# Layer 0's experts: one planner fixes each engine's order, context's output products are grouped, its rows are added as quarter rows, and GpSimd computes nothing there

## The chip, the cores and the metric

The kernel runs on one core of a Trainium2 chip. Its time is the device time of one execution in microseconds (us), as the median of three runs. One further execution was profiled; the rows below come from that one.

## The reference, cut to what matters

Two transformer layers over 1024 image tokens (`x`) and 256 context tokens (`ctx`), width 1024. Each layer ends in 16 experts. An expert takes the tokens with the highest affinity to it (128 of `x`, and in layer 0 also 32 of `ctx`), runs them through a gated hidden layer of 1024 and adds the gated result to their rows:

```python
cap = CAPACITY_FACTOR * t // N_EXPERTS
...
xs = jax.vmap(lambda hb, ib: hb[ib])(h, idx)
hid = jax.nn.silu(jnp.einsum('becd,edf->becf', xs, wg)) * jnp.einsum('becd,edf->becf', xs, wu)
ys = jnp.einsum('becf,efd->becd', hid, wd) * gates[..., None].astype(h.dtype)
return jax.vmap(lambda ib, yb: jnp.zeros((t, d), h.dtype).at[ib.reshape(-1)].add(yb.reshape(-1, d)))(idx, ys)
```

In layer 0 this is called for `x` and for `ctx` with the same expert weights; in layer 1 for `x` alone.

## The kernel before, in words

**Weights.** The three matrices of an expert (`wg`, `wu`, `wd`, 4 MB each in float32) come as six pieces of 2 MB, in the order wg0, wu0, wg1, wu1, wd0, wd1 (0 and 1 are the halves of the hidden width for wg and wu, of the hidden rows for wd). `Experts.dma` fetches a piece on SP's queue into one of three staging tiles `wst`. `Experts.split` cuts each into four units and makes two float16 tiles of a unit: ScalarE writes `wh` (L47), VectorE the rest `wl` (L55). There are 24 units in a ring, one expert's worth. So a staging tile is free when ScalarE and VectorE have split it, and a unit when TensorE has used it.

**One expert (`moe`, layer 0, 160 columns).** GpSimd gathers the token rows `xg` by indirect DMA (L80). TensorE transposes them (L92, 32 transposes `pt`, copied to `xT` at L94 by VectorE and ScalarE in turn). For each of eight blocks `f` of the hidden width, 48 products go into one PSUM tile `pgu` (L117, two tiles in rotation): float16 high and low parts of both factors, three terms. ScalarE computes silu into `sg` (L119), VectorE the product `hd` (L120), GpSimd the high part `hh` (L121) and the low part `hl` (L122). Then the output products: 24 steps (eight `f`, three terms). In each step come two products of 512 columns for the 128 image tokens (`py`, L138) and four of 256 columns for the 32 context tokens (`pc`, L141), each of which uses 32 of the array's 128 columns, side by side (`tile_position=(0,32*g)`). VectorE scales `py` into `ys` (two instructions, L147) and `pc` into `yc` (four instructions of 32 rows, L154), and GpSimd adds both to the tokens' rows `xr` and `cr` in memory by indirect DMA (L149, L155).

**What sets the order.** In this stage the framework's scheduler decides in which order each engine's instructions stand, from its own timeline; each engine has one list of its own. `Plan` (L936) is already in the kernel for another stage: work is handed to it as operations with an engine, a cost, what they read and write, a due time `v` and, for a PSUM tile, `get` and `free`. `Plan.order` is a list scheduler over those costs: among the operations that could start nearly as early as the earliest on an engine it takes the one with the lowest due time. `Plan.emit` records them in the resulting order and ties each instruction to the one before it on its engine.

Of the kernel before, what the change touches and what calls it, by code (L numbers as in the profile page):

```python
# [12 lines left out]
WS=256.0  # L13
CF=0
class Experts:
# [16 lines left out]
    def dma(self):  # L32
        e,m,c=self.todo.pop(0); nc=self.tc.nc
        p,r,NS=self.sts[self.m%len(self.sts)]; self.m+=1
# [36 lines left out]
def moe(tc, streams, E, ident, ahead=None, LD=5, fin=None):  # L71
# [3 lines left out]
    with tc.tile_pool(name="mx",bufs=2) as px, tc.tile_pool(name="mps",bufs=2,space=SP_) as ps, contextlib.ExitStack() as ec:  # L75
# [21 lines left out]
        if ahead: ahead()  # L97
        if len(streams)>1: pcp=ec.enter_context(tc.tile_pool(name="mpc",bufs=1,space=SP_,side="right"))
        xT=[t for t in turn(xg,True)][0]
        for e in range(nE):  # L100
# [30 lines left out]
            for ds in halves:
                for f in range(8):
                    if f%4==0 and ds[0]==0: E.upto(6*e+4+f//4+LD); D[f//4]=E.piece(e,2,f//4)
                    wh,wl=D[f//4][f%4]
                    n=0
                    for a,b in ((0,wh),(1,wh),(0,wl)):
                        for d in ds:
                            nc.tensor.matmul(py[d],hv[a][:,f,0:128],b[:,d*512:(d+1)*512],start=(f==0 and n==0),stop=(f==7 and n==2))  # L138
                        if pc is not None:
                            for g in range(4):  # L140
                                nc.tensor.matmul(pc[32*g:32*g+32,:],hv[a][:,f,128:160],b[:,g*256:(g+1)*256],start=(f==0 and n==0),stop=(f==7 and n==2),tile_position=(0,32*g))  # L141
                        n+=1
            def tokens():
# [6 lines left out]
            def context():  # L150
                s=streams[1]
                yc=px.tile([32,1024],F32,name="yc",bufs=1)
                for g in range(4):
                    last=nc.vector.scalar_tensor_tensor(yc[:,g*256:(g+1)*256],pc[32*g:32*g+32,:],s['gate'][32*g:32*g+32,e:e+1],s['g2'][32*g:32*g+32,g*256:(g+1)*256],op0=OP.mult,op1=OP.mult)  # L154
                return last,nc.gpsimd.indirect_dma_start(out=s['x'],out_offset=bass.IndirectOffsetOnAxis(ap=s['idx'][:,e:e+1],axis=0),in_=yc,in_offset=None,compute_op=OP.add)  # L155
# [780 lines left out]
class Plan:  # L936

    LAT=dict(PE=0.25,DVE=0.12,ACT=0.15,POOL=0.2,SP=2.7)
    def __init__(self,tc,kinds): self.tc,self.kinds,self.ops=tc,kinds,[]; self.W,self.R={},{}; self.last={}
# [507 lines left out]
```

## Time and profile before

| | us |
|---|---|
| median of three runs | 3189.5 (3186.51 to 3199.17) |
| the profiled execution | 3186.68 |
| its span, first to last instruction | 3184.9 |
| first to last add of `ys` in layer 0's experts | 427.6 to 1139.1 |

A row of the timeline gives the start, the duration, the engine, the line, the operation and its operands; `x4` is four instructions in one row. A row with PEld is a load of weights into the array, one with PE a product. Idle time before a row stands in brackets with what ended it.

### The profile page before, as it was taken

Reading aid. Unit: us, or ns where it says so; the run is one execution under the profiler, and the core shown is the slowest. Engines: PE = TensorE matmul, PEld = TensorE weight load, DVE = VectorE, ACT = ScalarE, POOL = GpSimd, SP = SyncE. Lnnn points to the kernel's source line nnn. Section 1 sums busy time; section 2 is a strip of 40 time slices with the busy share of each in tenths; the row PEclk is TensorE's granted clock in tenths of the full one; section 3 lists DMA queues with packets and bytes.
Section 4 is the critical chain, followed back from the end, with each engine's and each line's share of the span. In section 5 each row is a group of like instructions: output and inputs, shape, how many; then the busy total and the mean of one; then the engine's idle time right before and its main releaser. Section 6 shows DMA issues by size and latency. Waiting matters only on the chain.

```text
span 3184.9 us, 76806 instructions
## 1 busy us (share of the span) xinstructions
PE 2725.4 (86%) x31812; PEld 1968.7 (62%) x31812; DVE 2425.0 (76%) x4001; ACT 1965.4 (62%) x3386; POOL 1330.2 (42%) x1326
## 2 busy tenths in 40 slices
PE   3898499999999979998988689999758399888987
PEld 1323367667667644676655678888724177777775
DVE  4657877777776757688989588888788788778787
ACT  3214555555555547677656467777655677677775
POOL 4447343333433325566877100000000466566664
PEclk7899699999999989999875679999878699999999
DMA  6677788888888732322556746666445399999997
GB/s 243 233 264 247 263 319 281 296 302 284 300 303 271 250 109 109 120 69 72 176 160 180 141 82 115 125 118 128 135 154 198 135 353 347 334 338 348 352 347 264
DMA packets 468001, 705.63 MB, mean 222 GB/s; under 512 B 148889, under 2 KB 254781, under 8 KB 467650
## 3 DMA queue, kind: packets, MB, share of 16 engines
q1 hardware_dynamic: 451650, 644.08, 61.5%
q0 software_dynamic: 16000, 56.64, 6.5%
q8 instruction: 249, 4.08, 0.5%
q14 instruction: 102, 0.84, 0.1%
HBM read 596.21 MB, written 104.43 MB: 220 GB/s over the span
## 4 chain that ended last, share of the span: by engine, by line
PE 52%; DVE 18%; ACT 9%; DMA 8%; issue 6%; POOL 5%; SPq 0%; DVEq 0%; another core or an unknown queue 0%; POOLq 0%; ACTq 0%
PE pgu L117 18%; PE py L138 7%; PE pg L1033 4%; DVE wl L55 4%; PE pj L711 4%; DMA wst<-in_moe_wd 2%; POOL hh L121 2%; PE pc L141 2%; PE px L1126 2%; PE pm L1095 1%; PE opo L1293 1%; PE pj L798 1%; DMA adst<-in_ada_w 1%; ACT wh L47 1%; PE pt L92 1%
## 5 line engine op out<-in xcount | busy, mean ns | idle before, releaser
L117 PE MATMUL pgu<-xT,wh 128*128 128x160 f16 (+1 forms) x8192 | 815.9, 229 | 48.2 <-DVE hd L120 47.9
L55 DVE SCALAR_TENSOR_TENSOR wl<-wst,wh 128x1024 f16<-128x1024 f32 x601 | 777.0, 1343 | 101.3 <-ACT wh L47 100.7
L117 PE MATMUL pgu<-xT,wl 128*128 128x160 f16 (+1 forms) x4096 | 796.0, 229 | 2.1 <-DVE wl L55 1.1
L47 ACT ACTIVATE wh<-wst 128x1024 f16<-128x1024 f32 x648 | 638.6, 1047 | 167.2 <-PE pc L141 83.9
L117 PEld LDWEIGHTS <-wh 128*128 128x128 f16 x8192 | 674.3, 100 | 72.4 <-issue 51.9
L117 PEld LDWEIGHTS <-wl 128*128 128x128 f16 x4096 | 407.6, 100 | 9.6 <-DVE wl L55 3.4
L121 POOL CAST hh<-hd 128x160 f16<-128x160 f32 (+1 forms) x256 | 202.2, 825 | 488.3 <-DVE hd L120 488.1
L119 ACT ACTIVATE sg<-pgu 128x160 f32<-128x160 f32 (+1 forms) x256 | 69.4, 281 | 288.4 <-PE pgu L117 285.2
L711 PE MATMUL pj<-xj,wh 128*128 128x256 f16 x1152 | 216.7, 290 | 10.2 <-ACT ksq L833 4.5
L1033 PE MATMUL pg<-AG,BK 64*128 64x128 f32 (+1 forms) x1280 | 189.7, 315 | 12.7 <-DVE AG L1040 8.7
L120 DVE SCALAR_TENSOR_TENSOR hd<-pgu,sg 128x160 f32<-128x160 f32 (+1 forms) x256 | 73.0, 298 | 161.7 <-ACT sg L119 160.4
L122 POOL TENSOR_TENSOR hl<-hd,hh 128x160 f16<-128x160 f32 (+1 forms) x256 | 189.6, 756 | 9.5
L1033 PEld LDWEIGHTS pg<-AG,BK 64*128 64x128 f32 x1280 | 165.3, 217 | 27.5 <-DVE AG L1040 10.1
L711 PE MATMUL pj<-xj,wl 128*128 128x256 f16 x576 | 166.1, 290 | 0.7 <-DVE wl L653 0.7
L1037 ACT COPY GB<-pg 64x512 f32<-64x512 f32 (+1 forms) x320 | 126.9, 397 | 61.2 <-PE pg L1033 49.0
L138 PE MATMUL py<-wh,hh 128*128 128x512 f16 x512 | 154.8, 381 | 9.6 <-POOL hh L121 9.6
L138 PE MATMUL py<-wh,hl 128*128 128x512 f16 x512 | 155.3, 381 | 3.5 <-POOL hl L122 3.5
L138 PE MATMUL py<-wl,hh 128*128 128x512 f16 x512 | 155.8, 382 | 0.0
L688 DVE SCALAR_TENSOR_TENSOR xjf<-h,cols,xjf 128x252 f32<-128x252 f32 (+3 forms) x224 | 132.5, 619 | 29.1 <-POOL xjf L686 16.5
L1040 DVE TENSOR_TENSOR AG<-pg,gm 64x512 f32<-64x512 f32 (+1 forms) x160 | 101.5, 635 | 64.7 <-ACT GB L1037 60.9
L1058 POOL MEMSET R<- 128x1024 f32 (+1 forms) x20 | 11.2, 559 | 329.9 <-DVE At L1078 329.3
L52 POOL TENSOR_TENSOR wl<-wst,wh 128x1024 f16<-128x1024 f32 x47 | 101.2, 2164 | 105.2 <-ACT wh L47 105.1
(540 smaller groups left out, 5945.2 us busy)
## 6 DMA issues: line engine op xcount, KB each, us to landing
wst<-in_moe_wu SPq DMA_DIRECT2D x64, 2048.0 KB
wst<-in_moe_wg SPq DMA_DIRECT2D x48, 2048.0 KB
wst<-in_moe_wd SPq DMA_DIRECT2D x48, 2048.0 KB
adst<-in_ada_w SPq DMA_DIRECT2D x96, 512.0 KB
Dsc<-so SPq DMA_DIRECT2D x64, 512.0 KB
wsto<-in_moe_wg SPq DMA_DIRECT2D x16, 2048.0 KB
wsto<-in_moe_wd SPq DMA_DIRECT2D x16, 2048.0 KB
AG<-Dsc SPq DMA_DIRECT2D x64, 256.0 KB
```

Source lines behind the costliest of these rows:

```text
L47: with (self.tc.issue_after(self.last.ins) if pin and self.last else contextlib.nullcontext()): i=nc.scalar.activation(*a,**k)
L52: if eng is nc.gpsimd or (self.pool and self.n%self.pool==0): act(s,s,AF.Copy,scale=WS); act(h,s,AF.Copy); nc.gpsimd.tensor_sub(l,s,h)
L55: i=nc.vector.scalar_tensor_tensor(l,s,WS,h,op0=OP.mult,op1=OP.subtract)
L117: nc.tensor.matmul(p[:,m,:],a[:,o:o+128],xT[b][:,k,:],start=(n==0),stop=(n==23)); n+=1
L121: nc.gpsimd.tensor_copy(hh[:,f,:],hd)
L122: nc.gpsimd.tensor_sub(hl[:,f,:],hd,hh[:,f,:])
L138: nc.tensor.matmul(py[d],hv[a][:,f,0:128],b[:,d*512:(d+1)*512],start=(f==0 and n==0),stop=(f==7 and n==2))
L688: def acc(o,s): nc.vector.scalar_tensor_tensor(o,s,m,o,op0=OP.mult,op1=OP.add)
L711: nc.tensor.matmul(p,us[k][hf][a][:,o:o+128],xh[b][:,k],start=(c==0),stop=(c==23)); c+=1
L1033: ct=4*c4+j; nc.tensor.matmul(pg[:,128*j:128*j+N],BK[h,ct].rearrange("p a t -> p (a t)"),AG[h,par,ct,:N],start=True,stop=True,tile_positio ...
L1037: def ev(pg,h=h,cs=cs,par=par): nc.scalar.copy(GB[h,cs,:N],V4(pg)[h,:,:N]); q=slice(64*par+32,64*par+64); nc.scalar.copy(GB[q,cs,0:32],V4( ...
L1040: def mk(pg,o=o,par=par,cs=cs): nc.vector.tensor_mul(AG[o,par,cs,:N],V4(pg)[o,:,:N],gm[o,None,:N].to_broadcast([64,4,N]))
```

## The change

Layer 0 is computed by a new function `moe2`; `moe` keeps layer 1 and loses its context parts. `moe2` hands gathers, transposes, fetches (`SP`), splits, products and adds to a `Plan`, with due times built from an expert period `VP` and a step `VF` for each `f`. Three more things differ. The 24 steps of the output products become, for each half of `wd`, four operations of six `py` products each and then one operation `downc` with all 48 `pc` products of the half. `hh` goes to ScalarE and `hl` to VectorE; all `xT` copies go to ScalarE. `yc` has the shape 128 x 256 (row 32g+t holds quarter g of token t), so that one VectorE instruction scales it, and its add goes to `cr` seen as 1024 rows of 256, by an index `idx4` that holds four times the row plus the quarter. There are three `pgu` tiles, two `pt`, two `py` and one `pc`.

```diff
+def moe2(tc, streams, E, ident):
...
+        kinds=dict(pgu=[ps.tile([128,2,T],F32,name=f"pgu{i}") for i in range(3)],pt=[ps.tile([128,4,T],F16,name=f"pt{i}") for i in range(2)])
+        py=[ps.tile([128,512],F32,name=f"py{i}") for i in range(2)]; pc=ps.tile([128,256],F32,name="pc")
+        plan=Plan(tc,kinds); op=plan.op
...
+                a=op('PE',0.5,tr,r=[('xg',0,e%2),('xg',1,0)],v=v+n*VF,get='pt')
+                op('ACT',0.69,lambda pt,g=g,q=q: nc.scalar.copy(xT[e%2][:,g,q*4:q*4+4],pt),w=[('xT',e%2,n)],v=v-VF+n*VF,free=a)
+        VF=3.34; VP=42.0
...
+        def pieces(last,v):
...
+                    def ld(x=x,m=m,b=b): b['st']=E.fetch(x,m)
+                    op('SP',6.8,ld,w=[sk],v=v)
...
+                    op('ACT',1.05,hi,r=[sk],w=[('u',r,0)],v=v+0.2*u); op('DVE',1.23,lo,r=[sk,('u',r,0)],w=[('u',r,1)],v=v+0.2*u)
...
+                a=op('PE',3.33,gu,r=both(us[0]+us[1])+[('xT',e%2,n) for n in range(4)],v=v,get='pgu')
+                i=f%2
+                op('ACT',0.3,lambda p,i=i: nc.scalar.activation(sg[i],p[:,0,:],AF.Silu,scale=1/WS),r=[('a',a['i'])],w=[('sg',i)],v=v-100.0)['pre'].add(a['i'])
+                x=op('DVE',0.32,lambda p,i=i: nc.vector.scalar_tensor_tensor(hd[i],p[:,1,:],1/WS,sg[i],op0=OP.mult,op1=OP.mult),r=[('sg',i)],w=[('hd',i)],v=v-100.0,free=a)
+                plan.ops[x['i']-1]['src']=a
+                op('ACT',0.3,lambda e=e,f=f,i=i: nc.scalar.copy(hh[e%2][:,f,:],hd[i]),r=[('hd',i)],w=[('hh',e%2,f)],v=v-100.0)
+                op('DVE',0.3,lambda e=e,f=f,i=i: nc.vector.tensor_sub(hl[e%2][:,f,:],hd[i],hh[e%2][:,f,:]),r=[('hd',i),('hh',e%2,f)],w=[('hl',e%2,f)],v=v-100.0)
...
+                    def down(f=f,un=us[fq][0],hv=hv):
+                        for n,(a,b) in enumerate(((0,'h'),(1,'h'),(0,'l'))):
+                            for d in range(2): nc.tensor.matmul(py[d],hv(a,f)[:,0:128],un[b][:,d*512:(d+1)*512],start=(f==0 and n==0),stop=(f==7 and n==2))
+                    op('PE',1.3,down,r=both(us[fq:fq+1])+[('hh',e%2,f),('hl',e%2,f)],w=['py'],v=v0+28.5+1.6*f)
+                def downc(h=h,us=us,hv=hv):
+                    for f in range(4*h,4*h+4):
+                        un=us[f%4][0]
+                        for n,(a,b) in enumerate(((0,'h'),(1,'h'),(0,'l'))):
+                            for g in range(4): nc.tensor.matmul(pc[32*g:32*g+32,:],hv(a,f)[:,128:160],un[b][:,g*256:(g+1)*256],start=(f==0 and n==0),stop=(f==7 and n==2),tile_position=(0,32*g))
+                op('PE',1.35,downc,r=both(us)+[(n,e%2,f) for n in ('hh','hl') for f in range(4*h,4*h+4)],w=['pc'],v=v0+28.5+1.6*(4*h+3))
...
+            op('DVE',0.45,lambda e=e: nc.vector.scalar_tensor_tensor(yc,pc,sc['gate'][:,e:e+1],sc['g2'],op0=OP.mult,op1=OP.mult),r=['pc'],w=['yc'],v=v0-100.0)
...
+            nc.vector.tensor_scalar(s['idx4'],pg[:,16:32],4.0,gq,op0=OP.mult,op1=OP.add)
...
-            moe(tc,st,E,i16)
+            moe2(tc,st,E,i16)
```

In the first place TensorE is in the output products of expert 1. This stood there before, one step of 24: the end of a pair of `py` products, the four `pc` products, and the next `py`.

```order
L138 LDWEIGHTS hh_3757
L138 MATMUL py_4314<-wh8_3659,hh_3757 128x512
L141 LDWEIGHTS hh_3757
L141 MATMUL pc_4315<-wh8_3659,hh_3757 32x256
L141 LDWEIGHTS hh_3757
L141 MATMUL pc_4315<-wh8_3659,hh_3757 32x256
L141 LDWEIGHTS hh_3757
L141 MATMUL pc_4315<-wh8_3659,hh_3757 32x256
L141 LDWEIGHTS hh_3757
L141 MATMUL pc_4315<-wh8_3659,hh_3757 32x256
L138 LDWEIGHTS hl_3758
L138 MATMUL py_4313<-wh8_3659,hl_3758 128x512
```

This stands there in the changed kernel (expert 0, end of the second half): `py` products follow each other, and the `pc` products begin after the last of them.

```order
L231 MATMUL py0_3006<-wh8_2967,hl0_2989 128x512
L231 LDWEIGHTS hl0_2989
L231 MATMUL py1_3007<-wh8_2967,hl0_2989 128x512
L231 LDWEIGHTS hh0_2987
L231 MATMUL py0_3006<-wl8_2968,hh0_2987 128x512
L231 LDWEIGHTS hh0_2987
L231 MATMUL py1_3007<-wl8_2968,hh0_2987 128x512
L237 LDWEIGHTS hh0_2987
L237 MATMUL pc_3008<-wh8_2955,hh0_2987 32x256
```

Here 24 `py` stand in a row and then 48 `pc`, twice for each expert, where before the two kinds took turns 24 times.

In the second place VectorE is in expert 1's hidden blocks while it splits later pieces (`wl0`, `wl8`). Before:

```order
L120 SCALAR_TENSOR_TENSOR hd_4010<-pgu_3960,sg_4009 128x160
L120 SCALAR_TENSOR_TENSOR hd_4083<-pgu_4033,sg_4082 128x160
L55 SCALAR_TENSOR_TENSOR wl8_4168<-wst0_4165,wh8_4167 128x1024
L55 SCALAR_TENSOR_TENSOR wl8_4172<-wst0_4165,wh8_4171 128x1024
L55 SCALAR_TENSOR_TENSOR wl8_4176<-wst0_4165,wh8_4175 128x1024
L120 SCALAR_TENSOR_TENSOR hd_4150<-pgu_4100,sg_4149 128x160
L120 SCALAR_TENSOR_TENSOR hd_4233<-pgu_4183,sg_4232 128x160
L55 SCALAR_TENSOR_TENSOR wl8_4180<-wst0_4165,wh8_4179 128x1024
```

And in the changed kernel:

```order
L219 SCALAR_TENSOR_TENSOR hd0_2993<-pgu1_3002,sg0_2991 128x160
L195 SCALAR_TENSOR_TENSOR wl8_3900<-wst0_3667,wh8_3899 128x1024
L222 TENSOR_TENSOR hl1_2990<-hd0_2993,hh1_2988 128x160
L195 SCALAR_TENSOR_TENSOR wl8_3954<-wst0_3667,wh8_3953 128x1024
L219 SCALAR_TENSOR_TENSOR hd1_2994<-pgu2_3003,sg1_2992 128x160
L195 SCALAR_TENSOR_TENSOR wl0_4013<-wst0_3836,wh0_4012 128x1024
L222 TENSOR_TENSOR hl1_2990<-hd1_2994,hh1_2988 128x160
```

`hl` is now in VectorE's list, mostly one split after its `hd`; between the two ScalarE has to make `hh`. ScalarE's list at the same blocks shows what `hh` stands behind:

```order
L194 ACTIVATE wh8_3899<-wst0_3667 128x1024
L218 ACTIVATE sg0_2991<-pgu1_3002 128x160
L194 ACTIVATE wh8_3953<-wst0_3667 128x1024
L221 CAST hh1_2988<-hd0_2993 128x160
L218 ACTIVATE sg1_2992<-pgu2_3003 128x160
L194 ACTIVATE wh0_4012<-wst0_3836 128x1024
L221 CAST hh1_2988<-hd1_2994 128x160
```

Before, `hh` was in GpSimd's list; now it follows one split `wh` on ScalarE.

## Rows read from the trace of the kernel before

**Rows 1.** The page: busy time, share of the span and instructions of each engine.

```profile
PE 2725.4 (86%) x31812; PEld 1968.7 (62%) x31812; DVE 2425.0 (76%) x4001; ACT 1965.4 (62%) x3386; POOL 1330.2 (42%) x1326
```

**Rows 2.** Instructions on tile `ys`: durations (min/median/max, ns), first and last start.

```profile
L149 POOL DMA_INDIRECT xr<-ys,idxx x16: 1572/1625/1642, 427.6 to 1139.1; - x16
```

**Rows 3.** Stretches of one expert's length: busy us per engine, granted clock, DMA share, GB/s.

```profile
571.00:618.43 47.43, 46.74 (x560) 33.32 (x560) 34.27 (x40) 26.84 (x34) 19.06 (x20) 1.00 0.85 290
...
855.60:903.00 47.40, 47.39 (x564) 33.52 (x564) 34.47 (x40) 26.85 (x34) 15.65 (x20) 1.00 0.85 290
```

**Rows 4.** Groups by line and shape, 427 to 1140: busy us, mean ns, idle before.

```profile
L55 DVE SCALAR_TENSOR_TENSOR wl<-wst,wh 128x1024 f16<-128x1024 f32 x347 | 410.4, 1235 | 32.7 <-ACT wh L47 32.3
...
L47 ACT ACTIVATE wh<-wst 128x1024 f16<-128x1024 f32 x344 | 338.0, 1045 | 109.2 <-PE pc L141 83.9 <-DMA wst<-in_moe_wd 22.3
...
L121 POOL CAST hh<-hd 128x160 f16<-128x160 f32 x120 | 109.5, 980 | 288.6 <-DVE hd L120 288.6
...
L138 PE MATMUL py<-wh,hh 128*128 128x512 f16 x240 | 72.5, 384 | 6.8 <-POOL hh L121 6.8
...
L120 DVE SCALAR_TENSOR_TENSOR hd<-pgu,sg 128x160 f32<-128x160 f32 x120 | 36.8, 317 | 140.6 <-ACT sg L119 140.1
...
L119 ACT ACTIVATE sg<-pgu 128x160 f32<-128x160 f32 x120 | 34.0, 295 | 201.4 <-PE pgu L117 198.4 <-DVE hd L120 3.0
...
L154 DVE SCALAR_TENSOR_TENSOR yc<-pc,gatec,g 32x256 f32<-32x256 f32 x63 | 30.0, 476 | 0.7
...
L94 ACT COPY xT<-pt 128x640 f16<-128x640 f16 x28 | 19.2, 686 | 3.8 <-PE pt L92 3.8
...
L94 DVE COPY xT<-pt 128x640 f16<-128x640 f16 x28 | 13.4, 479 | 0.4 <-PE pt L92 0.4
```

**Rows 5.** Timeline of TensorE, output products of layer 0.

```profile
539.75 0.61 PE L138 MATMUL py<-wh,hh 128*128 128x512 f16 x2
540.29 0.29 PE L141 MATMUL pc<-wh,hh 128*32 128x256 f16 x4
540.51 0.60 PE L138 MATMUL py<-wh,hl 128*128 128x512 f16 x2
```

**Rows 6.** Timeline of TensorE, output products of layer 1, where there is no `pc`.

```profile
2706.24 0.59 PE L138 MATMUL py<-wh,hh 128*128 128x512 f16 x2
2706.67 0.59 PE L138 MATMUL py<-wh,hl 128*128 128x512 f16 x2
```

**Rows 7.** PEld timeline, a later stage that uses halves of the array's columns.

```profile
1885.80 1.01 PEld L1116 LDWEIGHTS px<-W,AG 128*64 128x64 f32 x30 [0.21 <-ACT W L1139]
```

**Rows 8.** PE timeline, the products to those loads.

```profile
1885.80 1.15 PE L1116 MATMUL px<-W,AG 128*64 128x64 f32 x30
```

**Rows 9.** The chain that ended last, pieces between 543 and 590.

```profile
564.84 4.66 POOL hh L121
...
569.55 0.60 PE py L138 x2
...
576.02 0.55 PE pt L92 x9
...
586.70 0.94 PE pt L92 x16
```

**Rows 10.** Timeline of VectorE at the end of the last expert.

```profile
1137.43 1.41 DVE L147 SCALAR_TENSOR_TENSOR ys<-py,gatex,g 128x512 f32<-128x512 f32 x2 [10.14 <-PE py L138]
1138.76 1.95 DVE L154 SCALAR_TENSOR_TENSOR yc<-pc,gatec,g 32x256 f32<-32x256 f32 x4
```

**Rows 11.** Timeline of GpSimd at the end of the last expert.

```profile
1139.12 1.57 POOL L149 DMA_INDIRECT xr<-ys,idxx  x1 [10.88 <-DVE ys L147]
1141.00 1.34 POOL L155 DMA_INDIRECT cr<-yc,idxc  x1 [0.31 <-DVE yc L154]
```

**Rows 12.** A stretch of expert 0 with columns as in rows 3.

```profile
385.00:405.00 20.00, 19.75 (x236) 16.71 (x236) 17.75 (x22) 14.44 (x19) 9.63 (x14) 0.91 1.04 387
```

**Rows 13.** SP's own waits, 428 to 1090: us in total, times, longest.

```profile
SPq L36 <- DVE wl L55: 253.6, 42, 10.5
```

More of the change, by code (lines that the diff above doesn't have):

```diff
@@ L32, in dma, with key, fetch @@
     def dma(self):
-        e,m,c=self.todo.pop(0); nc=self.tc.nc
-        p,r,NS=self.sts[self.m%len(self.sts)]; self.m+=1
+        x=self.todo.pop(0); self.m+=1; self.q.append((self.key(x),self.fetch(x,self.m-1)))
+    def key(self,x): return ('x' if x[1] is None else x[0],)+x[1:]
+    def fetch(self,x,n):
+        e,m,c=x; nc=self.tc.nc; p,r,NS=self.sts[n%len(self.sts)]
         st=p.tile([128,4096],F32,name=f"wst{r}",bufs=NS); w=(e if m is None else self.W[m][self.layer,e]).rearrange("(j p) f -> p j f",p=128)
@@ L97, in moe @@
         if ahead: ahead()
-        if len(streams)>1: pcp=ec.enter_context(tc.tile_pool(name="mpc",bufs=1,space=SP_,side="right"))
         xT=[t for t in turn(xg,True)][0]
@@ L138, in moe @@
                             nc.tensor.matmul(py[d],hv[a][:,f,0:128],b[:,d*512:(d+1)*512],start=(f==0 and n==0),stop=(f==7 and n==2))
-                        if pc is not None:
-                            for g in range(4):
-                                nc.tensor.matmul(pc[32*g:32*g+32,:],hv[a][:,f,128:160],b[:,g*256:(g+1)*256],start=(f==0 and n==0),stop=(f==7 and n==2),tile_position=(0,32*g))
                         n+=1
@@ L149, in tokens @@
                 nc.gpsimd.indirect_dma_start(out=s['x'],out_offset=bass.IndirectOffsetOnAxis(ap=s['idx'][:,e:e+1],axis=0),in_=ys,in_offset=None,compute_op=OP.add)
[L150 to L155, printed above, removed]
@@ L612, in finish @@
         s['gate']=gate; s['idx']=idx[0:cap]
+        if rep>1:
+            gq=pr.tile([128,1],F32,name="gq"+nm); s['idx4']=pr.tile([128,16],I32,name="idx4"+nm)
+            for r in range(rep): nc.vector.memset(gq[r*cap:(r+1)*cap],float(r))
+            nc.vector.tensor_scalar(s['idx4'],pg[:,16:32],4.0,gq,op0=OP.mult,op1=OP.add)
 CK=1
@@ L939, in __init__, with op @@
     def __init__(self,tc,kinds): self.tc,self.kinds,self.ops=tc,kinds,[]; self.W,self.R={},{}; self.last={}
-    def op(self,eng,us,fn,r=(),w=(),v=0.0,get=None,free=None,tag=None):
-        o=dict(i=len(self.ops),eng=eng,us=us,fn=fn,v=v,get=get,free=free,tag=tag,pre=set(),n=0,suc=[],t=0.0)
+    def op(self,eng,us,fn,r=(),w=(),v=0.0,get=None,free=None,tag=None,lat=None):
+        o=dict(i=len(self.ops),lat=self.LAT[eng] if lat is None else lat,eng=eng,us=us,fn=fn,v=v,get=get,free=free,tag=tag,pre=set(),n=0,suc=[],t=0.0)
         for x in r:
@@ L970, in order @@
             if o['get']: o['slot']=slots[o['get']].pop(0)[1]
-            done=end+self.LAT[e]
+            done=end+o['lat']
             if o['free']: p=o['free']; slots[p['get']].append([done,p['slot']]); slots[p['get']].sort()
@@ L1430, in load_g2 @@
     for s in streams:
-        g=pool.tile([128,1024],F32,name=f"g2{s['si']}"); nc.sync.dma_start(g,bcast(mods[s['si']:s['si']+1,5120:6144]))
+        row=mods[s['si']:s['si']+1,5120:6144]; n=1 if s['cap']==128 else 4; w=1024//n
+        g=pool.tile([128,w],F32,name=f"g2{s['si']}")
+        for r in range(n): nc.sync.dma_start(g[32*r:32*r+(128 if n==1 else 32)],bass.AP(tensor=row.tensor,offset=row.offset+r*w,ap=[[0,128//n],[1,w]]))
         nc.vector.tensor_scalar(g,g,1/WS,None,op0=OP.mult); s['g2']=g
```

85 lines of the change are left out of this document (75 added, 10 removed).

## The prediction

> **What bounds the kernel now.** I read the page first. TensorE is busy for 86% of the span [rows 1], but that averages over many stages, and this change touches one, so the rest was read there. The add of `ys` closes each expert: sixteen of them from 427.6 to 1139.1 [rows 2], so an expert takes (1139.1 - 427.6)/15 = 47.43 us. In stretches of just that length [rows 3] TensorE is busy for 46.74 to 47.39 us at the full granted clock of 1.00 (2.4 GHz), VectorE for 34.3 to 34.5, ScalarE for 26.8, GpSimd for 16 to 19, and the DMA engines to 0.85. So TensorE sets the pace here, and it hardly ever waits: in the groups by line the one idle time of weight is 6.8 us in about fifteen experts, before the first `py` product, for GpSimd's `hh` [rows 4]. What counts is therefore how many us of TensorE an expert needs, then whether another engine or the DMA comes up behind it when that number falls.
>
> **What the output products cost, and what grouping removes.** The timeline shows one step of 24 [rows 5]: a pair of `py` begins at 539.75, the four `pc` at 540.29, the next pair at 540.51. A step is 0.76 us, 0.54 up to the `pc` and 0.22 from there. In layer 1, where no `pc` stand between, a pair of `py` begins every 2706.67 - 2706.24 = 0.43 us [rows 6]. So a set of four `pc` products between pairs costs 0.76 - 0.43 = 0.33 us. The four run side by side, so their streaming is that of one product of 256 columns, half of a `py`: 0.43/4 = 0.108 us. The other 0.22 us of the step is the change to 32-column pieces of the array and back. Before, an expert pays it 24 times, and after, twice.
>
> What a set costs inside a group of twelve isn't in the trace for this shape. Its floor is the streaming, 0.108. Its ceiling is 0.22, the time from the `pc` to the next `py` [rows 5], in which the array also has to run empty. The nearest row is another stage that works in column pieces without leaving them: 30 recorded weight loads in 1.01 us and their 30 products in 1.15 us side by side [rows 7, 8], which is one pair every (1.15 - 0.22)/29 = 0.03 us if 0.22 is taken off for the last product's own length. There the loads of the next products go on while products run. Four such pairs are 0.12 us, a little over the streaming, and I take 0.116. An expert's output products then need 24 x 0.43 + 2 x 0.33 + 22 x 0.116 = 13.53 us where they need 24 x 0.76 = 18.24 now: 4.71 less. With the floor it is 4.9 and with the ceiling 2.4.
>
> A rule stands against this. The Trainium skill, in TensorE: Matmul & The Clock Gate, section Part 3: Packing small matmuls — row/col tiling, says that a weight load overlaps running products only when they use other row groups of the array; all four `pc` products and the next four use all 128 rows. By that rule each set would pay its load again, and the sum would go by the ceiling. Rows 7 and 8 use all rows too and do overlap, so I weigh it as a rival and not as the forecast.
>
> **The other edits on TensorE's path.** `hh` leaves GpSimd. In the chain one `hh` takes 4.66 us, and the `py` product after it starts late [rows 9]; the mean of 120 is 0.98 [rows 4]. On ScalarE the nearest row is `sg`, the same shape in 0.295 us [rows 4]. The wait is 6.8/15 = 0.45 us in an expert; it goes, since block 7's `hh` and `hl` are wanted only by the last pairs of the second half, some 10 us after block 7's products. If it stayed whole, the sum would be 7 us worse over sixteen experts. The transposes were done in one run of sixteen (0.94 us) and two short ones (nine in 0.55 us) [rows 9]; four runs of eight cost at most 4 x 0.55 instead of 0.94 + 2 x 0.55, so I add 0.2 us. Three `pgu` tiles instead of two cost nothing and give VectorE more time to free one.
>
> An expert: -4.71 - 0.45 + 0.2 = -4.96 us, so 42.47 us. Sixteen: -79.4 us. Expert 0 begins with transposes and splits that both kernels order alike, and I count it like the others.
>
> At the end, `ys` takes 1.41 us and the four `yc` 1.95, and the add to `cr` is issued at 1141.00, 3.57 us after `ys` began [rows 10, 11]. Now `ys` needs only `py` and runs beside the last `pc` group (11 x 0.116 + 0.33 = 1.6 us). GpSimd then issues the add of `ys` for 1.57 and after 0.31 the add of `yc`, some 2 us after TensorE's end: 1.5 us less, once. The quarter rows are 128 smaller packets instead of 32 of the same bytes, which I cost at nothing, since the add of 128 `ys` rows is issued in 1.57 us, no longer than that of 32 `yc` rows; were it twice as long to land, it would be some 5 us, once.
>
> **What must hide beside 42.5 us.** VectorE: 34.4 us [rows 3], less three `yc` (3 x 0.476) and two `xT` copies (2 x 0.479), plus eight `hl`. Their price lies between that of `hd`, 0.317, and that of `xT`, 0.479 [rows 4]; I take `hd`'s, for the same shape. That is 34.5 us, and 36 at the other end. ScalarE: 26.8 + 8 x 0.295 + 2 x 0.686 = 30.6 us. DMA: 0.85 x 47.43 = 40.3 us, the closest. But that share holds packets slowed by each other; in a stretch at full load [rows 12] 387 GB/s go through, at which an expert's 290 GB/s x 47.43 us = 13.8 MB take 35.5 us. So all three fit, the DMA by 2 to 7 us. GpSimd only issues DMAs.
>
> SP's queue waits on VectorE most of the time [rows 13]: a fetch starts when a staging tile has been split. In the changed order VectorE's 24 splits are spread through the expert (two stretches of eight beside the hidden blocks, eight beside the output products), so a tile comes free every 7 us and has 21 us until it must be split again, three fetches' worth.
>
> **Sum.** -79.4 - 1.5 = -81 us. The profiled execution took 3186.68 us with a span of 3184.9; that would become about 3106 and 3104. The median is 2.8 above the profiled execution, so 3189.5 - 81 = **3108 us**. Bounds of the costs alone: set at its floor 3105; with `hh`'s wait kept, twice the landing and transposes at 0.6 more an expert, 3108 + 7 + 5 + 10 = 3130.
>
> **Rivals.**
> The weight loads don't overlap inside a group: 22 x (0.22 - 0.116) = 2.3 us an expert, 37 in all, so 3145. For it, that no row shows this very shape; against it, rows 7 and 8. Chance 0.08.
> The staging tiles starve the DMA: now it is idle for 0.15 x 47.43 = 7.1 us of an expert. If that idle time stays while transfers run as fast as in the full stretch, an expert takes 35.5 + 7.1 = 42.6 us and nothing changes; if at today's pace, 47.4 and the gain is gone. Halfway is 45 us, a gain of 2.4 x 16 = 39, so about 3150. It decides from 5 us of idle time at a mean pace. For it, 40.3 busy us; against it, that TensorE, not the DMA, made SP wait. Chance 0.12, over 3125 to 3190.
> Slower: `hl` on VectorE waits for `hh` on ScalarE, which may stand behind a split `wh` of 1.05 us, and the splits behind `hl` wait too. VectorE has 42.5 - 34.5 = 8 us to spare over eight blocks, so 1 us of waiting a block is free, at 1.6 us it stands where the kernel is now, and beyond that it is slower. With two `wh` and the cast ahead, 2.4 us a block, an expert takes 53.7 us and the kernel about 3290. Against it, that in the order mostly one 1.2 us split stands between `hd` and `hl`, which covers most of this. Chance 0.03.
>
> **How the numbers follow.** The forecast, TensorE at 42 to 43.5 us an expert, gets 0.77, with its own range 3097 to 3130. Adding the rivals up to 3150 (the set's, and half of the DMA's) brings the range to 3097 to 3150, and what lies above is some 0.09. Nearly all of this is faster by over 0.5% (16 us, about what a measurement of this kernel can tell from no change): 0.94. Same 0.03, the end of the DMA's rival; slower 0.03.
>
> **What would show it.** In the profile after: adds of `ys` every 42.5 us; 24 `py` at 0.215 us each and then 48 `pc` in 1.6 us up to the next product, where 2.7 would be the first rival; VectorE near 34.5 and ScalarE near 30.6 us an expert; DMA share near 0.9. The prediction is wrong if TensorE's idle time in an expert exceeds 1 us: before `pgu` and after `wl` means staging or VectorE, before `py` and after `hl` the new chain.

## The result, and the profile after

The changed kernel takes 3113.3 us (3109.66 to 3114.91, 4 runs) against 3194.34 us for the kernel before beside it (3186.51 to 3203.83, 4 runs): a ratio of 0.9743, 95% interval 0.9712 to 0.9775, or 81.0 us less. The forecast was 3108 us, 81 less than the 3189.5 that three runs of the kernel before had given; the fourth run beside it moved that median to 3194.34. Its profiled execution took 3114.62 us with a span of 3112.8. The page, as in [rows 1]:

```profile
PE 2655.6 (85%) x31812; PEld 2000.5 (64%) x31812; DVE 2415.6 (78%) x4056; ACT 2013.7 (65%) x3544; POOL 1131.1 (36%) x1070
```

TensorE has 70 us less work with the same 31812 products, ScalarE 48 more, GpSimd 199 less. The instructions on `ys`, as in [rows 2], and two stretches of one expert, as in [rows 3] (the length, then the busy us and the instructions of TensorE, its weight loads, VectorE, ScalarE and GpSimd, then the granted clock, the DMA share and GB/s):

```profile
L243 POOL DMA_INDIRECT xr<-ys,idxx x16: 1554/1605/1626, 421.3 to 1049.3; - x16
```

```profile
588.40:630.47 42.07, 42.07 (x564) 35.03 (x560) 34.07 (x43) 30.64 (x45) 5.77 (x4) 1.00 0.96 332
...
756.70:798.80 42.10, 42.10 (x565) 35.06 (x562) 33.89 (x43) 29.73 (x44) 5.76 (x4) 1.00 0.90 305
```

An expert takes (1049.3 - 421.3)/15 = 41.87 us where it took 47.43, and TensorE is busy for all of it at the full granted clock. The DMA share rose from 0.85 to 0.90 and 0.96: the same weights in less time. The timeline of TensorE shows an expert's first `pc` group and what stands around it, as in [rows 5]:

```profile
411.45 0.59 PE L231 MATMUL py<-wl,hh 128*128 128x512 f16 x2
411.97 0.29 PE L237 MATMUL pc<-wh,hh 128*32 128x256 f16 x4
412.09 0.28 PE L237 MATMUL pc<-wh,hl 128*32 128x256 f16 x4
412.20 0.28 PE L237 MATMUL pc<-wl,hh 128*32 128x256 f16 x4
...
413.19 0.28 PE L237 MATMUL pc<-wl,hh 128*32 128x256 f16 x4
413.40 0.61 PE L231 MATMUL py<-wh,hh 128*128 128x512 f16 x2
413.84 0.59 PE L231 MATMUL py<-wh,hl 128*128 128x512 f16 x2
```

The twelve sets begin (413.19 - 411.97)/11 = 0.111 us apart, the group takes 413.40 - 411.97 = 1.43 us up to the next product, and a pair of `py` still takes 0.43. From the start of the last pair before the group to the next pair are 413.40 - 411.45 = 1.95 us, so a group adds 1.52 us to the `py`. The weights for the sets are loaded in the same stretch; one row of PEld from the middle of the group, and the loads of the stage:

```profile
412.10 0.22 PEld L237 LDWEIGHTS <-hh 128*32 128x32 f16 x8
```

```profile
L237 PEld LDWEIGHTS <-hh 128*32 128x32 f16 x960 | 25.5, 96 | 13.2 <-issue 12.7
```

A load takes 96 ns, and the 48 loads of a group still fit into its 1.43 us. The groups by line over the stage (busy, mean ns of one, idle before) show who makes `hh` and `hl` now, and what they wait for, as in [rows 4]:

```profile
L195 DVE SCALAR_TENSOR_TENSOR wl<-wst,wh 128x1024 f16<-128x1024 f32 x349 | 414.1, 1220 | 43.7 <-ACT wh L194 42.7
...
L194 ACT ACTIVATE wh<-wst 128x1024 f16<-128x1024 f32 x348 | 346.0, 1049 | 13.8 <-DMA wst<-in_moe_wd 9.0 <-DMA wst<-in_moe_wg 4.8
...
L231 PE MATMUL py<-wh,hh 128*128 128x512 f16 x240 | 71.7, 380 | 0.0
...
L221 ACT CAST hh<-hd 128x160 f16<-128x160 f32 x119 | 38.2, 321 | 10.7 <-DVE hd L219 10.6
L222 DVE TENSOR_TENSOR hl<-hd,hh 128x160 f16<-128x160 f32 x119 | 38.1, 321 | 11.0 <-ACT hh L221 11.0
```

The 6.8 us before `py` are gone, and `hl` waits for `hh` for 11.0/15 = 0.73 us in an expert. ScalarE waits for fetches for 13.8 us (before: 22.3 for `wd` alone), so it doesn't wait longer for the DMA than before. Most of SP's own waiting is still for VectorE, as in [rows 13]:

```profile
SPq L37 <- DVE wl L195: 292.4, 49, 7.9
```

At the end of the last expert, VectorE and GpSimd, as in [rows 10, 11]:

```profile
1047.58 1.41 DVE L240 SCALAR_TENSOR_TENSOR ys<-py,gatex,g 128x512 f32<-128x512 f32 x2 [10.24 <-PE py L231]
1049.24 0.48 DVE L242 SCALAR_TENSOR_TENSOR yc<-pc,gatec,g 128x256 f32<-128x256 f32 x1 [0.25 <-PE pc L237]
```

```profile
1049.27 1.55 POOL L243 DMA_INDIRECT xr<-ys,idxx  x1 [35.83 <-DVE ys L240]
1051.13 1.56 POOL L244 DMA_INDIRECT cr<-yc,idx4c  x1 [0.30 <-issue]
```

**Where the time is.** The last add to `cr` moved from 1141.00 to 1051.13, so the stage ends 89.9 us earlier, not 81. The span is only 72.1 us shorter: behind the stage lie 2061.7 us where 2043.9 lay, in code that the change doesn't touch. The number of instructions there is the same on every engine, before and after (columns as in [rows 3]):

```profile
1141.00:3184.90 2043.90, 1722.87 (x21358) 1339.40 (x21358) 1641.18 (x2944) 1417.85 (x2647) 856.52 (x872) 0.87 0.63 195
```

```profile
1051.13:3112.80 2061.67, 1734.97 (x21358) 1346.76 (x21358) 1640.17 (x2944) 1418.94 (x2647) 858.22 (x872) 0.86 0.63 193
```

Two pieces of that code, before and after, in stretches that hold nearly the same work:

```profile
1425.00:1455.00 30.00, 29.37 (x264) 25.65 (x263) 23.13 (x42) 26.24 (x71) 21.41 (x31) 0.98 0.01 1
1505.00:1535.00 30.00, 26.73 (x176) 17.39 (x176) 26.30 (x37) 19.09 (x49) 25.72 (x21) 0.83 0.56 174
```

```profile
1338.00:1373.00 35.00, 31.54 (x262) 27.07 (x261) 22.80 (x42) 26.42 (x70) 20.86 (x31) 0.90 0.01 1
1423.50:1457.50 34.00, 30.74 (x162) 18.73 (x161) 27.43 (x38) 18.54 (x46) 25.13 (x22) 0.65 0.55 173
```

The products are nearly as many (264 and 262, 176 and 162) and the busy time of VectorE and ScalarE is the same to a few per cent, but they ran at a granted clock of 0.90 instead of 0.98 and of 0.65 instead of 0.83: more of it at 1.2 GHz. These two alone are 9 us of the 17.8.

### The profile page after: what moved, and what is told of

Its sections match the earlier page's. It is cut to its first block, busy times and chain, and to the rows that moved or that the text cites. A ratio compares the mean times of both kernels' runs of the same rounds, so it can differ in the third digit from the quotient of the medians.

```text
span 3112.8 us, 76320 instructions
## 1 busy us (share of the span) xinstructions
PE 2655.6 (85%) x31812; PEld 2000.5 (64%) x31812; DVE 2415.6 (78%) x4056; ACT 2013.7 (65%) x3544; POOL 1131.1 (36%) x1070
## 4 chain that ended last, share of the span: by engine, by line
PE 31%; DVE 14%; ACT 8%; DMA 6%; issue 3%; POOL 2%; SPq 0%; DVEq 0%; ACTq 0%; POOLq 0%
PE pgu L117 6%; PE pg L1127 4%; PE pj L805 4%; DVE wl L56 3%; PE py L137 3%; PE opo L1387 2%; PE px L1220 2%; DMA wst<-in_moe_wd 1%; ACT wh L48 1%; PE pm L1189 1%; PE pj L892 1%; DMA wst<-in_moe_wu 1%; PE px L1227 1%; ACT GB L1181 1%; PE pg L1142 1%
## 5 line engine op out<-in xcount | busy, mean ns | idle before, releaser
L214 PE MATMUL pgu<-xT,wh 128*128 128x160 f16 x4096 | 433.2, 233 | 3.8 <-DVE hd L219 3.8
L214 PE MATMUL pgu<-xT,wl 128*128 128x160 f16 x2048 | 427.6, 233 | 0.0
L117 PE MATMUL pgu<-xT,wh 128*128 128x128 f16 x4096 | 378.3, 225 | 46.3 <-DVE hd L120 46.1
L194 ACT ACTIVATE wh<-wst 128x1024 f16<-128x1024 f32 x368 | 365.8, 1049 | 22.3 <-DMA wst<-in_moe_wd 13.0
L117 PEld LDWEIGHTS <-wh 128*128 128x128 f16 x4096 | 330.6, 101 | 65.7 <-issue 49.8
L117 PE MATMUL pgu<-xT,wl 128*128 128x128 f16 x2048 | 366.4, 225 | 2.1 <-DVE wl L56 1.1
L214 PEld LDWEIGHTS <-wh 128*128 128x128 f16 x4096 | 339.8, 98 | 8.7 <-issue 7.2
L121 POOL CAST hh<-hd 128x128 f16<-128x128 f32 x128 | 86.9, 685 | 165.1 <-DVE hd L120 164.9
L163 POOL DMA_INDIRECT xg<-HC,idxc x16 | 15.2, 952 | 357.8 <-PE pt L173 357.5
L805 PEld LDWEIGHTS <-wh 128*128 128x128 f16 x1152 | 119.5, 107 | 35.2 <-issue 13.6
```

Source lines behind the costliest of these rows:

```text
L117: nc.tensor.matmul(p[:,m,:],a[:,o:o+128],xT[b][:,k,:],start=(n==0),stop=(n==23)); n+=1
L194: nc.scalar.activation(un['h'],b['st'][:,u*1024:(u+1)*1024],AF.Copy,scale=WS)
L214: nc.tensor.matmul(p[:,m,:],un[a][:,o:o+128],xT[e%2][:,b,k,:],start=(n==0),stop=(n==23)); n+=1
L805: nc.tensor.matmul(p,us[k][hf][a][:,o:o+128],xh[b][:,k],start=(c==0),stop=(c==23)); c+=1
```

## The experiments

The theory behind the forecast: grouping takes 4.7 us of TensorE's time from an expert, `hh`'s move 0.45 of waiting, and the planned order keeps all else hidden. The rival: the order is what brings it, by taking waits away. The kernels of this table cross the parts of the change. The rows with the planner also hold what came with it: three `pgu` tiles, all `xT` copies on ScalarE and the quarter rows, of which only the last is taken apart below. The kernel before with nothing but `hh` and `hl` moved was not run. The ratios are to runs of the kernel before on the same chip.

| order by | `hh`, `hl` on | `pc` | us an expert | TensorE idle in it | ratio |
|---|---|---|---|---|---|
| scheduler (before) | GpSimd | 24 turns | 47.43 | 0.58 | 1 |
| planner (e1_turns) | ScalarE, VectorE | 24 turns | 46.77 | 0.09 | 0.9988 (0.9971 to 1.0005) |
| scheduler (e2_group_only) | GpSimd | grouped | 46.78 | 3.28 | 0.9984 (0.996 to 1.0008) |
| scheduler (e7_group_h) | ScalarE, VectorE | grouped | 42.65 | 0.38 | 0.9808 (0.9774 to 0.9842) |
| planner (e3_gpsimd_h) | GpSimd | grouped | 41.77 | 0.07 | 0.9736 (0.9695 to 0.9777) |
| planner (after) | ScalarE, VectorE | grouped | 41.87 | 0.01 | 0.9743 (0.9712 to 0.9775) |

An expert's time is the first to the last add of `ys` by 15, and the idle time what TensorE isn't busy for in that stretch; the stretches of the four new rows, in that order:

```profile
428.34:1129.85 701.51, 700.22 (x8351) 496.40 (x8349) 496.75 (x635) 435.44 (x643) 76.78 (x56) 1.00 0.82 283
```

```profile
430.46:1132.10 701.64, 652.46 (x8348) 521.08 (x8345) 501.44 (x587) 382.13 (x492) 264.54 (x296) 0.98 0.82 281
```

```profile
424.95:1064.72 639.77, 634.06 (x8271) 507.46 (x8268) 520.92 (x703) 410.16 (x610) 102.52 (x55) 1.00 0.91 308
```

```profile
421.60:1048.10 626.50, 625.44 (x8316) 520.05 (x8313) 482.64 (x517) 407.09 (x528) 291.83 (x295) 1.00 0.94 322
```

**The planner without the groups.** The kernel after, with the `pc` products in turns again:

```diff
                             for d in range(2): nc.tensor.matmul(py[d],hv(a,f)[:,0:128],un[b][:,d*512:(d+1)*512],start=(f==0 and n==0),stop=(f==7 and n==2))
-                    op('PE',1.3,down,r=both(us[fq:fq+1])+[('hh',e%2,f),('hl',e%2,f)],w=['py'],v=v0+28.5+1.6*f)
-                def downc(h=h,us=us,hv=hv):
...
                             for g in range(4): nc.tensor.matmul(pc[32*g:32*g+32,:],hv(a,f)[:,128:160],un[b][:,g*256:(g+1)*256],start=(f==0 and n==0),stop=(f==7 and n==2),tile_position=(0,32*g))
-                op('PE',1.35,downc,r=both(us)+[(n,e%2,f) for n in ('hh','hl') for f in range(4*h,4*h+4)],w=['pc'],v=v0+28.5+1.6*(4*h+3))
+                    op('PE',2.28,down,r=both(us[fq:fq+1])+[('hh',e%2,f),('hl',e%2,f)],w=['py','pc'],v=v0+28.5+1.6*f)
```

> The changed kernel with the pc products put back between the py products (24 turns for each expert); everything else, the planner too, stays. Theory 1 (the turns are nearly the whole gain): a step costs 0.76 us again, the output products 18.2 us instead of 13.4, an expert 42.07 + 4.8 = 46.9 us, TensorE still without idle time, and the kernel 77 us slower than the changed one, about as slow as before (ratio to before 0.997 to 1.003). Rival (the planner's order and hh and hl off GpSimd bring a good part): an expert takes 45 us or less, ratio to before under 0.99.

It took 3190.23 us against 3196.67, as the theory has it: all that the change holds beside the groups brings next to nothing, 0.66 us an expert or some 10 us in the trace, and no clear difference in the time. TensorE no longer waits and yet is busy for 700.22/15 = 46.68 us an expert, since a step costs what it did in [rows 5]:

```profile
643.27 0.61 PE L231 MATMUL py<-wh,hh 128*128 128x512 f16 x2
643.80 0.29 PE L232 MATMUL pc<-wh,hh 128*32 128x256 f16 x4
644.03 0.60 PE L231 MATMUL py<-wh,hl 128*128 128x512 f16 x2
```

From this kernel to the kernel after only the grouping differs: TensorE's work falls from 46.68 to 627.88/15 = 41.86 us, the 627.88 being its busy time between the adds of after. Grouping is worth 4.82 us.

**The groups without the planner.** The kernel before, in its `moe`:

```diff
-                        if pc is not None:
-                            for g in range(4):
-                                nc.tensor.matmul(pc[32*g:32*g+32,:],hv[a][:,f,128:160],b[:,g*256:(g+1)*256],start=(f==0 and n==0),stop=(f==7 and n==2),tile_position=(0,32*g))
                         n+=1
+                    if pc is not None and f%4==3:
+                        for k in range(f-3,f+1):
...
+                                for g in range(4):
+                                    nc.tensor.matmul(pc[32*g:32*g+32,:],hv[a][:,k,128:160],b[:,g*256:(g+1)*256],start=(k==0 and n==0),stop=(k==7 and n==2),tile_position=(0,32*g))
```

> The kernel before with one edit: the pc products of a half of wd are written after its py products, no planner, hh and hl on GpSimd, whole rows. The framework's scheduler cuts the groups: about five stretches of pc for each expert instead of 24. Theory 1 (TensorE's work sets the pace whoever orders it): 19 turns fewer at 0.21 us, 47.5 - 4.0 = 43.5 us an expert, ratio about 0.98. Rival (without the planner the other engines come up): TensorE waits again for hh, wl or pieces, 45 us or more an expert, ratio 0.987 or more.

It took 3191.89 us, no measurable difference: the theory's number failed, and the rival's held. TensorE's work did fall, to 652.46/15 = 43.50 us, but 3.28 us of waiting came in. The waits of TensorE in the stage (us in total, times, longest):

```profile
PE py L138 <- POOL hh L121: 36.2, 14, 4.9
PE pt L92 <- ACT xT L94: 10.9, 14, 0.8
```

One such wait on GpSimd, VectorE and TensorE:

```profile
842.61 5.78 POOL L121 CAST hh<-hd 128x160 f16<-128x160 f32 x1 [8.20 <-DVE hd L120]
```

```profile
842.46 5.75 DVE L55 SCALAR_TENSOR_TENSOR wl<-wst,wh 128x1024 f16<-128x1024 f32 x5
```

```profile
848.45 1.03 PE L138 MATMUL py<-wh,hh 128*128 128x512 f16 x2 [4.51 <-POOL hh L121]
849.41 0.40 PE L145 MATMUL pc<-wh,hh 128*32 128x256 f16 x4
```

The cast that takes 0.32 us alone began inside VectorE's run of five splits and ended with it. TensorE stood for 4.51 us, and its next products ran slower, 1.03 us for a pair that takes 0.59: in the 48.44 us around it the granted clock is 0.96. So GpSimd's lateness costs twice here, as a wait and as time at 1.2 GHz. The Trainium skill, in SBUF — State Buffer, section SBUF: two separate sides, says that VectorE with two inputs in SBUF and GpSimd share one pair of ports, taken by whichever starts first for its whole instruction, while the other stands still. The rows agree that GpSimd stood while VectorE split, but here it stood through five instructions and not one.

**The groups, `hh` and `hl` moved, no planner.** On top of the last edit, for layer 0:

```diff
-                nc.gpsimd.tensor_copy(hh[:,f,:],hd)
-                nc.gpsimd.tensor_sub(hl[:,f,:],hd,hh[:,f,:])
+                (nc.scalar.copy if len(streams)>1 else nc.gpsimd.tensor_copy)(hh[:,f,:],hd)
+                (nc.vector if len(streams)>1 else nc.gpsimd).tensor_sub(hl[:,f,:],hd,hh[:,f,:])
```

> The kernel before with the context products grouped (as in the second experiment) and hh on ScalarE, hl on VectorE in layer 0; no planner, the scheduler of the language still sets the order. Theory 1 (GpSimd's hh is what ate the gain of grouping alone: 36.2 us of waits before py in the stage): those waits go, experts of 44.5 us or less instead of 46.9, ratio to before 0.988 or lower. Rival (the scheduler's order is what eats it: it puts the output products right behind block 7, so TensorE waits for whichever engine makes hh and hl, and the casts now stand behind splits): TensorE still idle for 2 us or more an expert, experts of 46 us or more, ratio 0.995 or higher.

It took 3136.08 us (3135.54 to 3136.92) against 3197.15: the theory held, with more than its bound. By the two ratios, these two lines more give 56 us. TensorE's waits for `hh` are 3.4 us in the stage instead of 36.2. What is missing to the kernel after is 0.38 us of idle time and 42.27 - 41.86 = 0.41 us of work in an expert; the timeline shows the scheduler cutting an expert's 24 sets into some six groups of one to nine, each with its own change of pieces. Four more changes at 0.22 us would be 0.88, so this gives the direction of the 0.41 and not its size.

**The planner and the groups, `hh` and `hl` on GpSimd.** The kernel after, with two lines changed:

```diff
-                op('ACT',0.3,lambda e=e,f=f,i=i: nc.scalar.copy(hh[e%2][:,f,:],hd[i]),r=[('hd',i)],w=[('hh',e%2,f)],v=v-100.0)
-                op('DVE',0.3,lambda e=e,f=f,i=i: nc.vector.tensor_sub(hl[e%2][:,f,:],hd[i],hh[e%2][:,f,:]),r=[('hd',i),('hh',e%2,f)],w=[('hl',e%2,f)],v=v-100.0)
+                op('POOL',0.98,lambda e=e,f=f,i=i: nc.gpsimd.tensor_copy(hh[e%2][:,f,:],hd[i]),r=[('hd',i)],w=[('hh',e%2,f)],v=v-100.0)
+                op('POOL',0.58,lambda e=e,f=f,i=i: nc.gpsimd.tensor_sub(hl[e%2][:,f,:],hd[i],hh[e%2][:,f,:]),r=[('hd',i),('hh',e%2,f)],w=[('hl',e%2,f)],v=v-100.0)
```

> The kernel after, with hh and hl of layer 0 computed on GpSimd again, as before. Theory 1 (taking hh off GpSimd is a part of the gain, as the forecast counted it): TensorE waits for hh or hl at the output products at least as long as before, 0.45 us an expert, and up to the 2.3 us (36.2/16) of the kernel that only groups; experts of 42.5 to 44.4 us instead of 42.1, so 7 to 37 us slower than after, and GpSimd near 18 us an expert. Rival (the planned order alone hides GpSimd's lateness, since block 7's hh is wanted only by the last pairs): experts of 42.1 us, no wait of TensorE, the time of after within 0.3%.

It took 3107.45 us, the time of after: here the rival held. No output product waits for GpSimd. The casts (`hh`, min/median/max in ns; first the kernel before, then this one) are slower in the median, but the longest is 1.4 us where it was 4.65:

```profile
L121 POOL CAST hh<-hd x120: 316/785/4654, 433.2 to 1127.4; 128x160 f16<-128x160 f32 x120
```

```profile
L221 POOL CAST hh<-hd x119: 316/1241/1399, 432.3 to 1035.6; 128x160 f16<-128x160 f32 x119
```

So `hh`'s wait can be taken away in two ways, by another engine or by the planner with what came with it, and one is enough. Without either, the groups bring nothing that can be measured.

**Two staging tiles instead of three.** `E.stage(3)` becomes `E.stage(2)` and `E.ahead(9,...)` becomes `E.ahead(8,...)` in the kernel after.

> The kernel after with two staging tiles for the expert weights instead of three (one fetch fewer ahead at the start). Tests the staging rival of the prediction, and how near the DMA is to being the bound: its engines are busy for 0.89 to 1.00 of an expert of 42.1 us. Theory 1 (three tiles are just enough; a fetch that starts only when a tile has been split leaves the DMA idle with two): experts of 43.5 to 47 us, TensorE waits before pgu for wl, 20 to 75 us slower than after. Rival (two are enough, the splits are spread so that a fetch always has its tile): 42.1 us an expert and the time of after within 0.3%.

It took 3218.93 us (ratio 1.0072, 1.0048 to 1.0096), some 105 slower than after and beyond the theory's 75. The waits of TensorE and ScalarE in the stage, and the stretch of its 15 experts:

```profile
PE pgu L214 <- DVE wl L195: 45.8, 72, 0.9
```

```profile
ACT wh L194 <- DMA wst<-in_moe_wu: 125.9, 28, 6.8
ACT wh L194 <- DMA wst<-in_moe_wg: 44.8, 25, 3.6
```

```profile
444.50:1157.40 712.90, 659.27 (x8284) 537.99 (x8281) 493.70 (x638) 434.75 (x650) 89.46 (x56) 0.96 0.84 285
```

An expert takes 47.53 us, and the first add comes 23 us later. TensorE's idle time is 53.6 us of the stage; its busy time rose by 31 us too, at a granted clock of 0.96 instead of 1.00, and that part was not counted. This is the prediction's staging rival with its mechanism, one tile away from the changed kernel.

**One group an expert.** The kernel after, with `downc` once behind all 48 `py`:

```diff
-                def downc(h=h,us=us,hv=hv):
-                    for f in range(4*h,4*h+4):
-                        un=us[f%4][0]
+                if h==0: continue
+                def downc(us=U[e,2,0]+us,hv=hv):
+                    for f in range(8):
+                        un=us[f][0]
...
-                op('PE',1.35,downc,r=both(us)+[(n,e%2,f) for n in ('hh','hl') for f in range(4*h,4*h+4)],w=['pc'],v=v0+28.5+1.6*(4*h+3))
+                op('PE',2.67,downc,r=both(U[e,2,0]+us)+[(n,e%2,f) for n in ('hh','hl') for f in range(8)],w=['pc'],v=v0+28.5+1.6*(4*h+3))
```

> The kernel after with all 96 context products of an expert in one group after the 48 py products, instead of two groups of 48. Theory 1 (a group costs its sets at 0.110 us and one change of 0.22 us there and back): 0.2 us less an expert, adds of ys every 41.9 us, 3 us in all, ratio to before 0.001 lower than after's. Rival (the first half's four pairs of unit tiles are held some 6 us longer, the splits of the next pieces wait for them, and DMA and TensorE with them): TensorE idle before pgu, experts of 42.3 us or more, slower than after by 4 us or more.

It took 3105.7 us (ratio 0.9706, 0.9676 to 0.9736). The stretch of its 15 experts:

```profile
422.50:1048.20 625.70, 625.70 (x8379) 526.48 (x8371) 501.15 (x639) 436.38 (x648) 84.19 (x55) 1.00 0.94 322
```

41.71 us an expert, 0.15 less than after, and no wait of TensorE: the first theory holds in the trace. A second time, beside the kernel after:

> One group of 96 context products an expert, beside the kernel after on the same chip. Theory 1 (a change to 32-column pieces and back is 0.2 us, and an expert now has one instead of two): adds of ys 0.15 to 0.2 us closer, 2 to 3 us in all, which 5 rounds can hardly tell: ratios of the two within 0.003 of each other. Rival (something larger came with it, since the medians of the earlier runs lay 7.6 us apart): faster than after by 5 us or more again.

It took 3101.59 us (0.9711, 0.9683 to 0.9739) beside 3119.95 for after: 18 us less, where the stage again shows 2 to 3. Over all runs of both the medians are 3101.84 (11 runs) and 3114.91 (11 runs). So it has the lowest median of all versions, 13 us below after, of which the stage shows 2.3; beside e3_gpsimd_h, 3107.45 us on the same chip as the 3105.7, it is not clearly ahead. The first theory fails in the time, and the rest of the difference has no place in the traces: behind the stage its two traces take 2067 and 2060 us, as those of after do.

**Whole rows.** The kernel after with `yc` as four instructions of 32 rows and one add of 32 whole rows, as before:

```diff
...
-            op('DVE',0.45,lambda e=e: nc.vector.scalar_tensor_tensor(yc,pc,sc['gate'][:,e:e+1],sc['g2'],op0=OP.mult,op1=OP.mult),r=['pc'],w=['yc'],v=v0-100.0)
+            def con(e=e):
+                for g in range(4): nc.vector.scalar_tensor_tensor(yc[:,g*256:(g+1)*256],pc[32*g:32*g+32,:],sc['gate'][32*g:32*g+32,e:e+1],sc['g2'][32*g:32*g+32,g*256:(g+1)*256],op0=OP.mult,op1=OP.mult)
+            op('DVE',1.95,con,r=['pc'],w=['yc'],v=v0-100.0)
...
```

> The kernel after with the rows of context added whole again: four yc of 32 rows an expert instead of one of 128, one add of 32 rows of 1024 instead of 128 quarter rows. Theory 1 (the forecast priced the quarter rows at nothing on the way, and VectorE has some 8 us of an expert free): experts of 42.1 us as in after, VectorE 1.4 us busier an expert, the end of the stage 1 to 2 us later (three more yc before the last add), so 0 to 3 us slower in all. Rival (four times as many packets cost the DMA, which is busy for 0.9 to 1.0 of an expert): the DMA share of an expert falls by 0.02 or more, and the kernel is faster than after by 3 us or more.

It took 3113.0 us (0.9746, 0.972 to 0.9773), the time of after. Over the same 628.00 us VectorE is busy for 520.47 us instead of 499.37, 1.41 an expert, and the DMA share is 0.94 instead of 0.93; the queue of GpSimd's DMAs holds 16000 packets instead of 17536. From the first add of `ys` to the last of `cr` are 631.2 us, and 629.8, 630.8 and 630.9 in the three traces of after. So the quarter rows cost nothing that shows, and bring 0.3 to 1.4 us.

**Both kernels again, for the time behind the stage.**

> The kernel before, unchanged, with a second profile. In the first pair of profiles the changed kernel was 90 us ahead when layer 0's experts ended and 72 at the end. Theory 1 (TensorE's clock falls to its lower level at other moments from run to run, in stages that the change doesn't touch): from the last add of cr to the end this kernel takes another time than the 2044 us of the first profile, by several us, and more of it at the lower clock where it is longer. Rival (the change itself makes the later stages slower): this run repeats the first profile's later stages within 2 us.

> The changed kernel, unchanged, with a second profile. Theory 1: its later stages differ from the first profile's 2062 us by several us as well, towards either side. Rival: they take 2062 us again, 18 more than those of the kernel before.

> The kernel after once more, timed beside the next two kernels. Theory 1 (the stages behind the change hold the same work, and their length moves only with the time that TensorE spends at half clock in them): last add of cr at 1051 to 1053 us, and the rest of the span equals 1781 us plus half of the half-clock time in it, within 4 us, whatever that time is. Rival (the change itself lengthens a later stage, by data that come later or by an order that moved): the rest of the span exceeds 1785 us plus half of the half-clock time.

Spans of 3193.4 (before), 3119.6 and 3120.1 us (after), at mean clocks of 0.893, 0.885 and 0.885. Behind the last add of `cr` lie 2051.2, 2067.1 and 2063.9 us. Adding up the time at half clock in the granted clock's records there gives 528 and 535 us in the two traces of before, 559, 572 and 575 in the three of after; less half of that, the rest is 1780 and 1784, 1782, 1781 and 1776 us. In the last run the end of the stage, 1056.2, missed the expected 1053, for its first add was late already, and 1776 misses the 4 us by 0.6; the rival's 1785 is not reached. Over all 13 traces this rest is 1770 to 1787 us. So the later stages hold the same work, and in the five traces of the two kernels they differ mostly by time at 1.2 GHz. Over all 13 that is only a part of it: the rest is 17 us wide, and the later stages as they stand are 23 wide.

The 13 traces also fall into two groups. Where an expert takes 46.8 us or more (before twice, e1_turns, e2_group_only, e5_stage2), the later stages take 2044 to 2053 us, 2049 in the mean, with 528 to 549 us at half clock; in the eight with experts of 41.7 to 42.7 us they take 2051 to 2067, 2062 in the mean, with 541 to 575. This fits medians that are 81 us apart and not the stage's 90, and the rival, that the change itself lengthens what follows, is not excluded. Against it, the mean clock over all timed runs is 0.890 for before (41 runs) and 0.888 for after (11), which comes to about the same time at half clock in a whole execution. Why later stages with the same work take longer is thus not settled.

## Why the prediction was right, point by point

**The step's two parts.** The prediction took 0.22 us of each step for the change to 32-column pieces and back, and 0.116 for a set inside a group. The sets came 0.111 apart and the last one 0.21 before the next `py`. A group adds 1.52 us to the `py`, where 11 x 0.116 + 0.33 = 1.61 was forecast, and the saving is 4.82 us an expert, where 4.71 was. The first rival is out: the weights of `pc` are loaded (96 ns each) while products on the same 128 rows run. This goes against the sentence on row groups that the prediction took from the Trainium skill, TensorE: Matmul & The Clock Gate, section Part 3: Packing small matmuls — row/col tiling; the same section also lets a load into a background weight buffer run ahead, and no row here shows which buffer a load went to.

**`hh`.** The wait was counted at 0.45 us an expert, and all idle time that left is 0.57. Its price was right for the order of before and wrong as a part that adds: beside the groups in the scheduler's order the same wait is worth 36.2/15 = 2.4 us and more, in the planned order nothing. The slower rival, `hl` behind `hh` behind a split, is there with 0.73 us an expert, far below the 8 us at which it decides.

**The terms that were mis-sized.** Transposes and the rest were to cost 0.2 us more; the planner's other edits instead took 46.85 - 46.68 = 0.17 us of TensorE's work away (702.76/15 in the kernel before, with the turns in both); which of them did it was not taken apart. So an expert fell by 4.82 + 0.57 + 0.17 = 5.56 us, not 4.96. After TensorE's last product the add to `cr` comes 1051.13 - 1049.18 = 1.95 us later, "some 2 us" as forecast, against 1141.00 - 1137.83 = 3.17 before: 1.22 us less and not 1.5, since the forecast's 3.57 counts from the start of `ys` and its 2 from TensorE's end. Over sixteen experts and the end that makes the 89.9 us, 9 more than the sum.

**Staging.** The DMA is nearer to its limit than anything but TensorE, at 0.90 to 0.96, and yet TensorE waits for no fetch: its idle time over the fifteen experts is 0.12 us. The second rival is out for three tiles and true for two. VectorE at 34 and ScalarE at 30 us in the two stretches are near the forecast's 34.5 and 30.6.

**What the sum left out.** It held everything behind the stage to be unchanged. In work that is so, in time not: the profiled pair gives 17.8 us back there, and the medians, 81 apart beside the stage's 90, some 9. That the median came out at exactly 81 is two misses of the same size against each other, a stage mis-sized by 9 us and a rest that isn't constant. That part is luck.

## What to carry to other kernels

Products that use pieces of the array belong in groups: a change there and back was 0.22 us here, twice the streaming of the set it served. Such a saving on the bounding engine arrives only if what was hidden behind the longer time stays hidden, so look for the operand that is made last, and on which engine; moving it, or ordering around it, here decided whether the saving arrived at all. And a wait priced in the order of before says little about its price in another order: cross the parts before adding them.

## What the runs showed of the hardware

A cast on GpSimd of 128 x 160 takes 0.32 us alone; in the planned order it takes 1.24 us beside runs of one to three splits on VectorE, and in the scheduler's order 4.65 us beside a run of four and 5.78 beside one of five. What lets it in after the first split or keeps it out to the last, no run here shows. ScalarE does the cast in 0.321 us, and VectorE `hl`, the difference to it, in 0.321. Idle stretches of TensorE of 3.3 and 3.6 us an expert went with a granted clock of 0.98 and 0.96 in the stage, and in the second TensorE's busy time rose by 31 us, so there a wait cost more than its length. And stages in which nothing was changed varied by 23 us, 2043.9 to 2067.1, over the traces of the two kernels, with the time at half clock in them.
